# Stick-breaking scores from 128-row operands kept in place, the causal mask on VectorE, two gate columns earlier, and the squares of x summed on VectorE

## The chip, the cores and the metric

The kernel runs on one core of a Trainium2 chip. The metric is the device time of one execution in microseconds. Before the change it is 1577.78 us, the median of three runs (1577.75 to 1578.48).

In the profile PE is TensorE's matmuls, PEld its weight loads, DVE is VectorE, ACT ScalarE, POOL GpSimd and SP SyncE, which here issues most of the DMAs.

## The reference

The kernel computes one decoder block on x of 1024 tokens by 1024 channels in float32. Two mixers, stick-breaking attention (8 heads of 64) and HGRN2 (4 heads of 128), work on projections of the normalized x; sigmoid gates merge them; an output projection and a SwiGLU FFN with residuals follow. Cut to what matters here:

```python
xn = rms_norm(x, norm1_g)
proj = xn @ w_in
q_sb, k_sb, v_sb, q_hg, f_hg, i_hg, g_hg, gate_sb, gate_hg = split_cols(proj, IN_SIZES)
q = rms_norm(heads(q_sb), q_norm_g)
k = rms_norm(heads(k_sb), k_norm_g)
# stick-breaking attention, in blocks of 128 queries
z = jnp.einsum('bhtd,bhsd->bhts', qb, kb).astype(jnp.float32) * scale
causal = s_idx < t_idx
sp = jnp.where(causal, jax.nn.softplus(z), 0.0)
rest = lax.cumsum(sp, axis=3, reverse=True) - sp
w = jnp.where(causal, jnp.exp(jax.nn.log_sigmoid(z) - rest), 0.0)
outs.append(jnp.einsum('bhts,bhsd->bhtd', w.astype(vb.dtype), vb))
...
mixed = jax.nn.sigmoid(gate_sb) * y_sb + jax.nn.sigmoid(gate_hg) * y_hg
h = x + mixed @ w_out
ffn = (jax.nn.silu(hn @ w_gate) * (hn @ w_up)) @ w_down
return h + ffn
```

## The kernel before

**Precision by splitting.** Everything is kept transposed, channels on the 128 partitions and tokens along the free dimension, in two halves of 512 tokens (h = 0, 1). TensorE works on fp32r operands. To keep float32 accuracy an operand is split into a high part (rounded to fp32r) and a low part (what is left), and a product is three matmuls: high by high, high by low, low by high. So a projection column of 128 output channels is, for each half, 8 contraction tiles of three matmuls of 512 columns (tiles oh, ol for the weights, ah, al for x, pj for the PSUM bank).

**The first stage and its planner.** The stage that ends before line 782 computes the input projections and both mixers. Its instructions aren't issued in the order in which the code names them: each helper (A for ScalarE, V for VectorE, G for GpSimd, M and T for TensorE, L for a DMA on SP's queue; lines 363 to 388) records an operation with an estimated cost, and `Plan.issue` (line 124) then orders each engine's operations by a rank, and within a rank by the length of the chain of work that still hangs on them. All are issued from line 182, so the profile shows L182 for the whole stage, and groups are told apart by their tiles. The order of each engine is thus fixed when the program is built, and an engine that meets an operation whose inputs aren't ready waits there.

**Filler.** Projection columns have the lowest rank (`proj`, line 478): TensorE takes them when nothing else is ready. They form one fixed sequence, the `fill` list, built from the strings in `FILL` (line 30), one string for each of four steps u. In a string "a" stands for the q, k and v columns of the next pair of attention heads, "g" for the HGRN2 output gate of head u, "i", "f" and "q" for the other HGRN2 columns of the next head, and "G" for one of the 16 columns of the merging gates. A gate column's result is copied out of PSUM by ScalarE and stored to DRAM (sig_d) by a DMA that ScalarE issues; it is needed in the next stage. The q, k and v columns of pair u have to wait (`gate`, line 776) for marks that the pair before sets, "free q" and "free k".

**Scores** (`take`, line 516, and `scores`, line 564). Two heads of 64 channels share a tile of 128 partitions. For q each head e has a tile qs (128 by 1024): the head's own 64 partitions hold the high part of q, the other 64 hold the low part. k is split into hk and lk, where each head's 64 rows lie in its own half. For a head's scores, SP issues two DMAs that copy the head's 64 rows of hk into both halves of a tile ks. A block of scores z (128 queries by up to 512 keys) is then two matmuls: qs against ks, 128 rows deep, which gives (high q + low q) by high k; and the 64 own rows of qs against the 64 rows of lk, 64 rows deep, which gives high q by low k. A block on the diagonal has a third matmul between them, 128 columns, of an identity against a tile `never`, which adds -2^100 where the key isn't before the query. There are 96 blocks in all, 64 of them on the diagonal. Each is followed by ScalarE's Abs, Relu, Exp and Ln, a scan and a subtraction on VectorE, and ScalarE's Exp.

**Sum of squares** (`take_x`, line 445). x comes in eight tiles for each half. ScalarE squares each; the first square goes to a tile acc (shown as tail). GpSimd adds four further squares to acc for the first half and three for the second, VectorE adds up the rest and joins them. A matmul of ones against acc (ms<-tail,ones) sums over partitions, and from it comes rr, the factor that every projection result is multiplied by as it leaves PSUM.

**After the first stage** the attention and HGRN2 outputs are read back from DRAM (o_d), split, and projected (lines 787 to 823), then come the output projection and the FFN.

Of the kernel before, what the change touches and what calls it, by code (L numbers as in the profile page):

```python
# [26 lines left out]
EPS = 1e-6  # L27
NEG = -float(2.0**100)
LEVELS = [64, 32, 16, 8, 4, 2, 1]
FILL = ["GgGaifq", "gaGfiqGG", "gaGGGiqGfGG", "gGGGGG"]  # L30
BANKS = [3, 2, 3]
WARM = 9
ORDER = [1, 6, 2, 5, 7, 4, 3]
# [169 lines left out]
def hybrid_block(ctx: ExitStack, tc, xT, wi, wb, wo, wg, wu, wd, vec, outT):  # L203
# [41 lines left out]
    rst = ExitStack()  # L245
    rrp = rst.enter_context(tc.tile_pool(name="rrp", bufs=1, side="right"))
    c1 = ExitStack()
    const1 = c1.enter_context(tc.tile_pool(name="const1", bufs=1, side="right"))
    ident = const1.tile([P, P], F32, name="ident")
    ones_r = const.tile([P, P], F32R, name="ones_r")  # L250
    bones_r = const1.tile([P, P], F32R, name="bones_r")
    never = const1.tile([P, P], F32R, name="never")
    ident_r = const1.tile([P, P], F32R, name="ident_r")
    eps_t = const.tile([P, 1], F32, name="eps_t")
    one_t = const.tile([P, 1], F32, name="one_t")
    qg = const.tile([P, 1], F32, name="qg")
# [8 lines left out]
    def setup(sp):  # L265
        make_identity(nc, ident)
        t2 = sp.tile([P, P], F32, tag="t2", name="t2")
        nc.vector.memset(t2, 0.0)
        nc.vector.memset(t2[0:64, 0:64], 1.0)
        nc.vector.memset(t2[64:128, 64:128], 1.0)  # L270
        nc.vector.tensor_copy(bones_r, t2)
        nc.vector.tensor_copy(ident_r, ident)
        t3 = sp.tile([P, P], F32, tag="t3", name="t3")
        nc.gpsimd.memset(t3, NEG)
        nc.gpsimd.affine_select(
            out=t3, in_=t3, pattern=[[1, P]], compare_op=ALU.is_ge, fill=0.0,
            base=0, channel_multiplier=-1)
        nc.vector.tensor_copy(never, t3)
        nc.vector.tensor_scalar(qg, vt[:, V_Q:V_Q + 1], 0.125, None, op0=ALU.mult)
        l0, l1 = vt[:, V_LB:V_LB + 4], vt[:, V_LB + 4:V_LB + 8]  # L280
        mx = sp.tile([P, 4], F32, tag="mx", name="mx")
        e0 = sp.tile([P, 4], F32, tag="e0", name="e0")
        e1 = sp.tile([P, 4], F32, tag="e1", name="e1")
        nc.vector.tensor_tensor(mx, l0, l1, op=ALU.max)
        nc.vector.tensor_tensor(e0, l0, mx, op=ALU.subtract)
        nc.vector.tensor_tensor(e1, l1, mx, op=ALU.subtract)
        nc.scalar.activation(e0, e0, AF.Exp)
        nc.scalar.activation(e1, e1, AF.Exp)
        nc.vector.tensor_tensor(e1, e0, e1, op=ALU.add)
        nc.vector.reciprocal(e1, e1)  # L290
        nc.vector.tensor_tensor(lb, e0, e1, op=ALU.mult)
        nc.vector.tensor_scalar(omlb, lb, -1.0, 1.0, op0=ALU.mult, op1=ALU.add)
        nc.vector.tensor_scalar(nomlb, omlb, -1.0, None, op0=ALU.mult)
# [31 lines left out]
    nc.vector.memset(ones, 1.0)  # L325
    nc.vector.tensor_copy(ones_r, ones)
    setup(pp)
    pre.close()


# [2 lines left out]
    for i in range(WARM):  # L333
        nc.tensor.matmul(warm.rearrange("p (o t) -> p o t", t=P), ones_r, wide, start=i == 0,
                         stop=i == WARM - 1)


    plan = Plan()
# [6 lines left out]
        wpool: dict(w=2, oh=4, ol=4),  # L345
        psum: dict(pj=BANKS[0], z=BANKS[1], ms=BANKS[2]),
        tmpp: dict(tmp=2),
        stk: dict(hk=1, lk=1, qs=3, ks=2, vx=1, vv=1),
        att: dict(aa=8, th=2, tl=2, ww=7, ot=2, pvt=1),
        hgp: dict(xf=2, xq=2, xi=2, xg=2, kb=4, dl=2, tail=4, ql=2,  # L350
                  state=5, bl=2),
    }
# [2 lines left out]
    def new(tag, shape=(P, HALF), dt=F32):  # L355
        pool, cap = where[tag]
        plan.ring(tag, cap)
        return Buf(tag, lambda: pool.tile(list(shape), dt, tag=tag, bufs=cap, name=tag))
# [13 lines left out]
    def G(fn, *args, us, rank=0, after=(), holds=(), **kw):  # L372
        return plan.op("G", us, [(fn, args, kw)], rank, after, holds=holds)
# [71 lines left out]
    def take_x(h):  # L445
        ss, acc, ws, sqs = new("ms"), new("tail"), [[], []], []
        for k in range(KT):
            x = new("aa" if h == 0 else ("xf", "xq", "xi", "xg")[k // 2])
            load(x, xT[k][:, hs(h)], 256)
            if h == 0 and k in (0, 1, 3, 4):  # L450
                u, i = k % 3, k // 3
                n, v = fill[u]
                w = new("kb")
                load(w, wi[COL[n] + v][:, hs(i)], 256)
                ws[u].append(split_w(w))
            g = vt[:, V_N1 + k:V_N1 + k + 1]
            A(act, xh[k][h][:, hs(h)], x, AF.Copy, scale=g, aps=1, rank=2 - h)
            V(stt, xl[k][h][:, hs(h)], x, g, xh[k][h][:, hs(h)].bitcast(F32), op0=ALU.mult,
              op1=ALU.subtract, aps=1, rank=2 - h)
            if k == 0:  # L460
                A(act, acc, x, AF.Square, rank=1 - h)
            else:
                sq = new("ww")
                A(act, sq, x, AF.Square, rank=1 - h)
                sqs.append(sq)
        nv = 3 + h
        for sq in sqs[:7 - nv]:
            G(nc.gpsimd.tensor_tensor, acc, acc, sq, op=ALU.add, us=1.5, after=(last_split[0],))
        for sq in sqs[8 - nv:]:
            V(tt, sqs[7 - nv], sqs[7 - nv], sq, op=ALU.add, rank=1 - h)  # L470
        V(tt, acc, acc, sqs[7 - nv], op=ALU.add, rank=1 - h)
        M(2048, [(ss, ones, acc, True, True)])
        rstd(rr[h], ss, D, rank=1 - h)
        return ws
# [33 lines left out]
        V(stt, x, x, g, sq, op0=ALU.mult, op1=ALU.mult, aps=1)  # L508
        return x

    half = [slice(0, 64), slice(64, 128)]

    heads = [dict() for _ in range(4)]
    gains = {"q": qg, "k": vt[:, V_K:V_K + 1]}
# [1 line left out]
    def take(nm, u, h, ps):  # L516

        d = heads[u] if nm != "G" else None
        if nm == "q":
            x = qk_in(ps, gains[nm], h)  # L520
            if h == 0:
                d[nm] = [new("qs", (P, S), F32R) for _ in range(2)]
            for e, t in enumerate(d[nm]):
                hi, lo = t[half[e]][:, hs(h)], t[half[1 - e]][:, hs(h)]
                A(nc.scalar.copy, hi, x[half[e]], part=True)
                V(tt, lo, x[half[e]], hi.bitcast(F32), op=ALU.subtract, part=True)
        elif nm == "k":
            x = qk_in(ps, gains[nm], h)
            if h == 0:
                d[nm] = (new("hk", (P, S), F32R), new("lk", (P, S), F32R))  # L530
            hi, lo = d[nm][0][:, hs(h)], d[nm][1][:, hs(h)]
            A(nc.scalar.copy, hi, x, part=True)
            V(tt, lo, x, hi.bitcast(F32), op=ALU.subtract, part=True)
        elif nm == "v":
            if h == 0:
                d["v"] = new("vx", (P, S))
            V(tt, d["v"][:, hs(h)], ps, rr[h], op=ALU.mult, part=True)
        elif nm == "G":
            x = new("tmp")
            A(nc.scalar.copy, x, ps, ps=True)  # L540
            plan.op("A", 0.1, [(nc.scalar.dma_start, (sig_d[u][:, hs(h)], x), {})], lat=2.5)
        elif nm == "hi":
            y, x = new("tmp"), new("xi")
            V(tt, y, ps, rr[h], op=ALU.mult)
            tp = new("ms")
            T([(tp[:, c * P:(c + 1) * P], y[:, c * P:(c + 1) * P]) for c in range(4)],
              holds=(x,))
            A(nc.scalar.copy, x, tp, ps=True)
            d[nm, h] = x
        elif nm == "hf":  # L550
            y, x = new("tmp"), new("xf")
            V(tt, y, ps, rr[h], op=ALU.mult)
            sigmoid(x, y)
            d[nm, h] = x
        else:
            x, s = new("x" + nm[1]), new("tmp")
            V(tt, x, ps, rr[h], op=ALU.mult)
            sigmoid(s, x)
            V(tt, x, s, x, op=ALU.mult)
            d[nm, h] = x  # L560
# [3 lines left out]
    def scores(j, last):  # L564
        d = heads[j]
        for e in range(2):
            qs, ks, kl = d["q"][e], new("ks", (P, S), F32R), d["k"][1][half[e]]
            for b in range(2):
                d["free k"] = L(ks[half[b]].bitcast(F32), d["k"][0][half[e]].bitcast(F32), 256,
                                part=True, land=3.5)  # L570
            for tb in range(8):
                n = (tb + 1) * P
                prev = None
                for c0, c1 in [(0, n)] if n <= 512 else [(512, n), (0, 512)]:
                    w = c1 - c0
                    z = new("z")
                    zw = z[:, :w]
                    q = qs[:, tb * P:(tb + 1) * P]
                    diag = c1 == n
                    mms = [(zw, q, ks[:, c0:c1], True, False),  # L580
                           (zw, qs[half[e]][:, tb * P:(tb + 1) * P], kl[:, c0:c1], False, True)]
                    if diag:
                        mms.insert(1, (z[:, w - P:w], ident_r, never, False, False))
                    last = M(2 * w + P * diag, mms, after=(last,))
                    a, c, y = new("aa"), new("aa"), new("ww")
                    aw, cw, yw = a[:, :w], c[:, :w], y[:, :w]
                    A(act, aw, zw, AF.Abs, n=w, ps=True)
# [8 lines left out]
                    A(act, yw, yw, AF.Exp, n=w)  # L596
                    d["w", e, tb, c0 // 512] = y
            if e == 0:
                d["free q"] = last
        return last  # L600

    def values(j, last):
# [530 lines left out]
```

## Time and profile before

| | us |
|---|---|
| median of the runs | 1577.78 |
| profiled execution, whole | 1582.62 |
| its span | 1580.9 |
| from the start to the first scores | 57 |
| first to last score block | 57.2 to 625 |
| last store of a mixer's output | 693.6 |
| next stage's first matmuls | 744.4 |

The span is what the trace covers; the execution's own time is 1.7 us longer. A row of the order of instructions gives the start, the length, the engine, the line, the operation with "out<-in", the shapes and the count of instructions merged into the row. Matmuls are pipelined, so a matmul's length in the trace is longer than its share of the engine: what TensorE spends on one is read from its start to the start of the next. In "128*64" style shapes the first factor is the depth (rows of the array in use) and the second the columns of weights; "128x512" is the moving operand.

### The profile page before, as it was taken

What the parts mean: (1) busy time and instruction counts of PE and PEld (TensorE: products, weight loads), DVE (VectorE), ACT (ScalarE), POOL (GpSimd) and SP (SyncE); (2) the same over time, 40 slices, a digit from 0 to 9 for tenths busy, and PEclk for the clock granted to TensorE, in tenths of its full rate; (3) what the DMA queues carried; (4) which work ended last, traced back from release to release, by engine and by line L of the source; (5) the groups of instructions that cost most, each with busy time, mean ns of one, the idle gap of its engine ahead of it and who ended that gap; (6) DMA issues with size and microseconds to landing.
All of it is one profiled execution on the core that took longest, in us unless ns stands there. A gap on an engine that the chain in (4) does not pass through costs nothing.

```text
span 1580.9 us, 20525 instructions
## 1 busy us (share of the span) xinstructions
PE 1554.4 (98%) x7277; PEld 1252.4 (79%) x7277; DVE 1173.6 (74%) x1968; ACT 792.0 (50%) x1479; POOL 185.7 (12%) x207
## 2 busy tenths in 40 slices
PE   8999999999999999999999989999999999999999
PEld 5788777878788777888888868777778888778887
DVE  8798778977887667973666799888887777566553
ACT  6675768577656778462333363332233333244442
POOL 6111201101111001122441210000000000000000
PEclk9999999999999999999999999999999999999999
DMA  4211121112111311153333454666643333587672
GB/s 171 70 38 42 55 68 30 43 44 70 51 36 55 87 47 52 63 202 126 131 122 124 143 162 165 213 213 213 213 160 107 107 107 107 209 301 218 195 222 93
DMA packets 79686, 192.72 MB, mean 122 GB/s; under 512 B 9312, under 2 KB 11360, under 8 KB 78176
## 3 DMA queue, kind: packets, MB, share of 16 engines
q1 hardware_dynamic: 74976, 183.03, 35.9%
q10 hardware_dynamic: 4608, 8.39, 1.5%
q8 instruction: 57, 0.93, 0.2%
q14 instruction: 45, 0.37, 0.1%
HBM read 131.61 MB, written 55.57 MB: 118 GB/s over the span
## 4 chain that ended last, share of the span: by engine, by line
PE 81%; DVE 10%; DMA 4%; issue 2%; ACT 1%; POOL 1%; SPq 0%; DVEq 0%; ACTq 0%; POOLq 0%
PE pj L182 27%; PE f L921 19%; PE ms L182 9%; PE f L1067 4%; PE f L1069 4%; PE f L1065 4%; PE z L182 4%; PE pj L303 2%; PE pj L304 2%; PE pj L305 2%; DMA w<-wu 1%; DVE ol L238 1%; PE z L304 1%; PE z L303 1%; PE z L305 1%
## 5 line engine op out<-in xcount | busy, mean ns | idle before, releaser
L182 PE MATMUL pj<-ah,oh 128*128 128x512 f32 x704 | 290.2, 412 | 1.6 <-POOL oh L182 1.6
L182 PE MATMUL pj<-ah,ol 128*128 128x512 f32 x704 | 276.7, 393 | 0.4 <-DVE ol L182 0.4
L182 PE MATMUL pj<-al,oh 128*128 128x512 f32 x704 | 275.9, 392 | 0.9 <-DVE al L182 0.8
L921 PE MATMUL f<-fh,oh 128*128 128x512 f32 x616 | 244.2, 396 | 5.7 <-DVE g L981 2.1
L921 PE MATMUL f<-fl,oh 128*128 128x512 f32 x616 | 243.4, 395 | 0.7 <-DVE fl L851 0.7
L921 PE MATMUL f<-fh,ol 128*128 128x512 f32 x616 | 243.1, 395 | 0.0
L237 ACT CAST oh<-w 128x512 fp32r<-128x512 f32 x168 | 102.4, 620 | 197.9 <-PE f L921 128.4
L182 PEld LDWEIGHTS pj<-ah,oh 128*128 128x128 f32 x704 | 133.1, 189 | 31.1 <-issue 6.1
L182 PEld LDWEIGHTS pj<-ah,ol 128*128 128x128 f32 x704 | 132.5, 188 | 30.7 <-DVE ol L182 1.3
L182 PEld LDWEIGHTS pj<-al,oh 128*128 128x128 f32 x704 | 133.5, 190 | 23.4 <-DVE al L182 1.6
L921 PEld LDWEIGHTS f<-fh,oh 128*128 128x128 f32 x616 | 115.4, 187 | 37.1 <-DVE g L981 4.2
L238 DVE TENSOR_TENSOR ol<-w,oh 128x512 fp32r<-128x512 f32 x168 | 113.9, 685 | 40.6 <-ACT oh L237 40.3
L921 PEld LDWEIGHTS f<-fl,oh 128*128 128x128 f32 x616 | 115.5, 187 | 28.8 <-DVE fl L851 1.0
L921 PEld LDWEIGHTS f<-fh,ol 128*128 128x128 f32 x616 | 115.5, 187 | 28.2
L182 DVE TENSOR_TENSOR_SCAN aa<-aa,ww 128x512 f32<-128x512 f32 (+3 forms) x96 | 92.8, 981 | 45.8 <-ACT aa L182 34.5
L1065 PE MATMUL f<-bh,ah 128*128 128x512 f32 x296 | 114.8, 392 | 3.3 <-ACT bh L237 3.3
L1067 PE MATMUL f<-bl,ah 128*128 128x512 f32 x296 | 116.7, 394 | 1.3 <-DVE bl L238 1.3
L1069 PE MATMUL f<-bh,al 128*128 128x512 f32 x296 | 116.6, 394 | 0.0
L182 POOL TENSOR_SCALAR oh<-w 128x512 fp32r<-128x512 f32 x84 | 65.1, 775 | 426.4 <-PE pj L182 350.6
L238 DVE TENSOR_TENSOR al<-ra,ah 128x512 fp32r<-128x512 f32 x73 | 50.4, 691 | 74.8 <-ACT ah L237 74.8
L237 ACT CAST ah<-ra 128x512 fp32r<-128x512 f32 x73 | 45.5, 623 | 104.5 <-PE f L1067 103.9
L182 DVE TENSOR_TENSOR ol<-w,oh 128x512 fp32r<-128x512 f32 x84 | 59.0, 703 | 26.5 <-POOL oh L182 26.4
(276 smaller groups left out, 3025.9 us busy)
## 6 DMA issues: line engine op xcount, KB each, us to landing
w<-wi SPq DMA_DIRECT2D x42, 512.0 KB, 3.6
rb<-act_d SPq DMA_DIRECT2D x73, 256.0 KB, 4.3
w<-wg SPq DMA_DIRECT2D x22, 512.0 KB, 4.1
w<-wu SPq DMA_DIRECT2D x22, 512.0 KB, 4.1
w<-wd SPq DMA_DIRECT2D x22, 512.0 KB, 6.7
wd_d<-ds SPq DMA_DIRECT2D x44, 256.0 KB, 5.3
act_d<-c SPq DMA_DIRECT2D x11, 1024.0 KB, 3.9
act_d<-bs SPq DMA_DIRECT2D x44, 256.0 KB, 3.3
```

The costliest lines, as they stand in the source:

```text
L182: fn(*[a.real() if isinstance(a, View) else a for a in args], **{k: v.real() if isinstance(v, View) else v for k, v in kw.items()})
L237: pin(nc.scalar.copy(hi, src))
L238: pin(nc.vector.tensor_tensor(lo, src, hi.bitcast(F32), op=ALU.subtract))
L303: nc.tensor.matmul(out, hi[:, ws], a[ka][0][:, hs(h)], start=first and i == 0, stop=False)
L304: nc.tensor.matmul(out, hi[:, ws], a[ka][1][:, hs(h)], start=False, stop=False)
L305: nc.tensor.matmul(out, lo[:, ws], a[ka][0][:, hs(h)], start=False, stop=last and i == n - 1)
L921: nc.tensor.matmul(out, a[i][:, ws], bl[k][j], start=start and k == 0 and i + j == 0, stop=k == 3 and i == 1, skip_group_check=True)
L1065: nc.tensor.matmul(bank[d], hi[:, ws], bh, start=first and p == 0, stop=False, skip_group_check=True)
L1067: nc.tensor.matmul(bank[d], hi[:, ws], bl, start=False, stop=False, skip_group_check=True)
L1069: nc.tensor.matmul(bank[d], lo[:, ws], bh, start=False, stop=p == NP - 1, skip_group_check=True)
```

## The change

1. The score operands become six tiles that live through the stage. For each head e of a pair, qhh holds the high part of q in both halves, qlz the low part of q in the own half and zeros in the other, khl the high part of k in the own half and the low part in the other. The two matmuls of a block are qhh against khl (high q by high k plus high q by low k) and qlz against khl (low q by high k), both 128 rows deep. The DMA copies of k go. The tiles are single: the next pair overwrites them. ScalarE's copies for q become two for each head and half, and k is split by head.
2. The mask is no longer a matmul: VectorE writes -2^100 into the diagonal block of z in PSUM by a predicated copy, ahead of ScalarE's Abs and Relu.
3. In `FILL` one gate column moves into step 0 and one into step 1, both from the last step. "free k" is now set with "free q", after the first head's scores.
4. VectorE adds all squares of x; GpSimd adds none.
5. The buffers follow: hk, lk, qs and ks go, the ring aa grows from 8 to 10.

```diff
-FILL = ["GgGaifq", "gaGfiqGG", "gaGGGiqGfGG", "gGGGGG"]
+FILL = ["GgGGaifq", "gGaGfiqGG", "gaGGGiqGfGG", "gGGG"]
...
+    qkp = c1.enter_context(tc.tile_pool(name="qkp", bufs=1, side="right"))
...
-    never = const1.tile([P, P], F32R, name="never")
-    ident_r = const1.tile([P, P], F32R, name="ident_r")
+    future = const1.tile([P, P], I8, name="future")
+    never = const1.tile([P, P], F32, name="never")
...
-        nc.vector.tensor_copy(ident_r, ident)
-        t3 = sp.tile([P, P], F32, tag="t3", name="t3")
-        nc.gpsimd.memset(t3, NEG)
+        nc.vector.memset(never, NEG)
+        nc.gpsimd.memset(future, 1.0)
         nc.gpsimd.affine_select(
-            out=t3, in_=t3, pattern=[[1, P]], compare_op=ALU.is_ge, fill=0.0,
+            out=future, in_=future, pattern=[[1, P]], compare_op=ALU.is_ge, fill=0.0,
             base=0, channel_multiplier=-1)
-        nc.vector.tensor_copy(never, t3)
...
+    half = [slice(0, 64), slice(64, 128)]
+    qhh, qlz, khl = [[qkp.tile([P, S], F32R, name=f"{n}{e}") for e in range(2)]
+                     for n in ("qhh", "qlz", "khl")]
+    for e, t in enumerate(qlz):
+        nc.gpsimd.memset(t[half[1 - e]].bitcast(F32), 0.0)
     pre.close()
...
-        stk: dict(hk=1, lk=1, qs=3, ks=2, vx=1, vv=1),
-        att: dict(aa=8, th=2, tl=2, ww=7, ot=2, pvt=1),
+        stk: dict(vx=1, vv=1),
+        att: dict(aa=10, th=2, tl=2, ww=7, ot=2, pvt=1),
...
-        nv = 3 + h
-        for sq in sqs[:7 - nv]:
-            G(nc.gpsimd.tensor_tensor, acc, acc, sq, op=ALU.add, us=1.5, after=(last_split[0],))
-        for sq in sqs[8 - nv:]:
-            V(tt, sqs[7 - nv], sqs[7 - nv], sq, op=ALU.add, rank=1 - h)
-        V(tt, acc, acc, sqs[7 - nv], op=ALU.add, rank=1 - h)
+        for sq in sqs:
+            V(tt, acc, acc, sq, op=ALU.add, rank=1 - h)
         M(2048, [(ss, ones, acc, True, True)])
...
-        if nm == "q":
+        if nm in ("q", "k"):
             x = qk_in(ps, gains[nm], h)
-            if h == 0:
-                d[nm] = [new("qs", (P, S), F32R) for _ in range(2)]
-            for e, t in enumerate(d[nm]):
-                hi, lo = t[half[e]][:, hs(h)], t[half[1 - e]][:, hs(h)]
-                A(nc.scalar.copy, hi, x[half[e]], part=True)
-                V(tt, lo, x[half[e]], hi.bitcast(F32), op=ALU.subtract, part=True)
-        elif nm == "k":
-            x = qk_in(ps, gains[nm], h)
-            if h == 0:
-                d[nm] = (new("hk", (P, S), F32R), new("lk", (P, S), F32R))
-            hi, lo = d[nm][0][:, hs(h)], d[nm][1][:, hs(h)]
-            A(nc.scalar.copy, hi, x, part=True)
-            V(tt, lo, x, hi.bitcast(F32), op=ALU.subtract, part=True)
+            for e in range(2):
+                own, oth = half[e], half[1 - e]
+                hi = (qhh if nm == "q" else khl)[e]
+                A(nc.scalar.copy, hi[own][:, hs(h)], x[own], part=True)
+                lo = qlz[e][own] if nm == "q" else khl[e][oth]
+                V(tt, lo[:, hs(h)], x[own], hi[own][:, hs(h)].bitcast(F32), op=ALU.subtract,
+                  part=True)
+                if nm == "q":
+                    A(nc.scalar.copy, hi[oth][:, hs(h)], x[own], part=True)
...
         for e in range(2):
-            qs, ks, kl = d["q"][e], new("ks", (P, S), F32R), d["k"][1][half[e]]
-            for b in range(2):
-                d["free k"] = L(ks[half[b]].bitcast(F32), d["k"][0][half[e]].bitcast(F32), 256,
-                                part=True, land=3.5)
...
-                    mms = [(zw, q, ks[:, c0:c1], True, False),
-                           (zw, qs[half[e]][:, tb * P:(tb + 1) * P], kl[:, c0:c1], False, True)]
+                    mms = [(zw, q[e][:, tb * P:(tb + 1) * P], khl[e][:, c0:c1], q is qhh, q is qlz)
+                           for q in (qhh, qlz)]
+                    last = M(2 * w, mms, after=(last,))
                     if diag:
-                        mms.insert(1, (z[:, w - P:w], ident_r, never, False, False))
-                    last = M(2 * w + P * diag, mms, after=(last,))
+                        V(nc.vector.copy_predicated, z[:, w - P:w], future, never, n=P)
...
             if e == 0:
-                d["free q"] = last
+                d["free q"] = d["free k"] = last
```

More of the change, by code (lines that the diff above doesn't have):

```diff
@@ L335, in hybrid_block @@
                          stop=i == WARM - 1)
+    future = future.bitcast(U8)
     plan = Plan()
@@ L509, in qk_in @@
         return x
-    half = [slice(0, 64), slice(64, 128)]
+    qhh, qlz, khl = [[fixed(t) for t in ts_] for ts_ in (qhh, qlz, khl)]
     heads = [dict() for _ in range(4)]
@@ L577, in scores @@
                     zw = z[:, :w]
-                    q = qs[:, tb * P:(tb + 1) * P]
                     diag = c1 == n
-                    mms = [(zw, q, ks[:, c0:c1], True, False),
-                           (zw, qs[half[e]][:, tb * P:(tb + 1) * P], kl[:, c0:c1], False, True)]
+                    mms = [(zw, q[e][:, tb * P:(tb + 1) * P], khl[e][:, c0:c1], q is qhh, q is qlz)
+                           for q in (qhh, qlz)]
+                    last = M(2 * w, mms, after=(last,))
                     if diag:
-                        mms.insert(1, (z[:, w - P:w], ident_r, never, False, False))
-                    last = M(2 * w + P * diag, mms, after=(last,))
+                        V(nc.vector.copy_predicated, z[:, w - P:w], future, never, n=P)
                     a, c, y = new("aa"), new("aa"), new("ww")
```

## The prediction

> **What bounds the kernel now.** I read the page first, then a table of windows cut where the stages change, then the order of TensorE's instructions around single score blocks.
>
> ```profile
> span 1580.9 us, 20525 instructions
> PE 1554.4 (98%) x7277; PEld 1252.4 (79%) x7277; DVE 1173.6 (74%) x1968; ACT 792.0 (50%) x1479; POOL 185.7 (12%) x207
> ```
> ```profile
> core 0: us, PE busy (x) PEld busy (x) DVE busy (x) ACT busy (x) POOL busy (x), PEclk, DMA share, GB/s
> 0.00:57.00 57.00, 47.83 (x171) 34.41 (x171) 49.02 (x78) 33.13 (x57) 32.19 (x47) 0.94 0.44 142
> 57.00:640.00 583.00, 580.77 (x3024) 466.69 (x3025) 457.90 (x834) 419.18 (x861) 75.05 (x98) 1.00 0.18 52
> 640.00:694.00 54.00, 53.60 (x331) 46.09 (x330) 48.04 (x107) 26.62 (x48) 6.40 (x11) 1.00 0.22 67
> 694.00:744.00 50.00, 50.00 (x222) 41.36 (x221) 19.01 (x18) 20.67 (x26) 17.16 (x14) 1.00 0.59 208
> 744.00:1581.00 837.00, 822.20 (x3536) 663.86 (x3534) 599.60 (x932) 292.35 (x487) 54.94 (x38) 1.00 0.51 168
> ```
> From 57 us, where the scores begin, TensorE has work in every slice: it lacks 2.2 us of 583, then 0.4 of 54, then nothing. So a microsecond taken out of TensorE's own stream before 744 us should come off the time, as long as the others keep up. But busy is not the same as streaming, and the order shows the difference. Here is a score block off the diagonal, and one on it, each followed by a projection (pj):
>
> ```profile
> 201.52 0.39 PE L182 MATMUL pj<-ah,ol 128*128 128x512 f32 x1
> 201.75 0.39 PE L182 MATMUL z<-ks,qs 128*128 128x512 f32 x1
> 202.07 0.49 PE L182 MATMUL z<-lk,qs 64*128 64x512 f32 x1
> 202.49 0.50 PE L182 MATMUL pj<-ah,oh 128*128 128x512 f32 x1
> 202.83 0.40 PE L182 MATMUL pj<-al,oh 128*128 128x512 f32 x1
> ```
> ```profile
> 225.78 0.28 PE L182 MATMUL ms<-th,vv 128*128 128x256 f32 x1
> 225.90 0.28 PE L182 MATMUL ms<-tl,vv 128*128 128x256 f32 x1
> ...
> 231.72 0.28 PE L182 MATMUL z<-ks,qs 128*128 128x256 f32 x1
> 231.84 0.22 PE L182 MATMUL z<-never,ident_r 128*128 128x128 f32 x1
> 231.99 0.38 PE L182 MATMUL z<-lk,qs 64*128 64x256 f32 x1
> 232.30 0.50 PE L182 MATMUL pj<-ah,oh 128*128 128x512 f32 x1
> 232.64 0.39 PE L182 MATMUL pj<-al,oh 128*128 128x512 f32 x1
> ```
> Read the starts. A 512-column matmul that is 128 rows deep is followed after 0.23 us (201.52 to 201.75), a 256-column one after 0.12 (225.78 to 225.90). Around the 64-row matmul the steps are 0.32, 0.42 and 0.34 instead of 0.23 each: there are pauses going into it, in it and coming out of it. The mask matmul (never) is 128 rows deep and follows its neighbour at the normal 0.12; the pause comes only with the 64-row step behind it.
>
> **The scores on TensorE.** From 201.75 to 202.83 three 512-column matmuls take 1.08 us; at 0.23 each they are 0.69, so the pauses cost 0.39. From 231.72 to 232.64 it is 0.92 against 2 x 0.12 + 0.23 = 0.47: 0.45 for pauses and mask together.
>
> ```profile
> L182 PE MATMUL z<-lk,qs x96: 322/467/502, 57.5 to 625.4; 64*128 64x512 f32 x48, 64*128 64x128 f32 x16, 64*128 64x256 f32 x16, 64*128 64x384 f32 x16
> L182 PE MATMUL z<-never,ident_r x64: 219/222/278, 57.3 to 616.8; 128*128 128x128 f32 x64
> ```
> There are 96 blocks, 64 with a mask. 32 x 0.39 + 64 x 0.45 = 41 us; I take 42, since two blocks in a row and the narrow ones lie slightly higher. The new pair of matmuls (qhh then qlz against khl) is 128 rows deep both times and has the same columns as the old pair, so all of this goes if depth is the cause. The mask's own part of it is small: 64 x (0.45 - 0.39), 4 us.
>
> The Trainium skill speaks against this. In "TensorE: Matmul & The Clock Gate", section "Why this matters for your kernels", a single matmul of small depth takes the same time as one of 128 rows. By that rule the sum would hold only the mask. The rows above disagree: they show 0.32 and 0.42 where 0.23 is normal.
>
> **What takes the mask's place.** 64 predicated copies of 128 columns go to VectorE.
>
> ```profile
> L182 DVE COPY_PREDICATED kb<-mk,ms x48: 411/440/745, 108.9 to 682.2; 96x256 f32<-96x256 uint8 x8, 112x256 f32<-112x256 uint8 x8, 120x256 f32<-120x256 uint8 x8, 124x256 f32<-124x256 uint8 x8
> L182 DVE TENSOR_TENSOR ww<-z,aa 128x128 f32<-128x128 f32 x16 | 4.5, 280 | 0.1
> L182 ACT CAST qs<-aa x16: 604/618/626, 47.7 to 484.3; 64x512 fp32r<-64x512 f32 x16
> L182 DVE TENSOR_TENSOR lk<-aa,hk x8: 677/693/693, 44.1 to 528.8; 128x512 fp32r<-128x512 f32 x8
> ```
> The existing copies do 256 columns in 0.44 us; a 128-column VectorE operation on the same bank takes 0.28. The price of one lies between 0.28 and 0.44; I take 0.28, as the columns match: 18 us in all, up to 28. Building the operands adds 16 copies for q and 8 for k on ScalarE (24 x 0.62 = 15 us) and 8 subtractions for k on VectorE (8 x 0.69 = 5.5). Neither engine sets the pace: from 57 to 744 us VectorE is busy 458 + 48 + 19 = 525 us of 687. Afterwards it is about 549 of 645, 85%. ScalarE: 467 + 15 of 645, 75%. So this costs nothing directly, but the cover gets thinner, and each predicated copy waits for its matmuls in VectorE's queue. Behind it stand scans, weight splits (ol) and the emptying of pj banks; ScalarE's Abs waits for it, and TensorE for the banks.
>
> ```profile
> ACT aa L182 <- PE z L182: 27.3, 52, 5.3
> ```
> So far ScalarE waits 27 us in total for scores: that is room in hand. 42 us of TensorE time go, so up to 15 us more than this room may turn into TensorE waits; at best they stay at the 2.6 us of now. With the tail below I add 9, bounds 0 and 25.
>
> **What leaves the queues.** The 16 copies of k that SP issued, each with weight loads behind it, are gone.
>
> ```profile
> L182 SPq DMA_DIRECT2D ks<-hk x16: 476/587/1313, 52.6 to 530.6; - x16
> ```
> That is 16 x 0.59 = 9 us of SP's issuing. TensorE fills such waits with projections, so I count zero.
>
> **The two gate columns.** Each is 48 matmuls, 48 x 0.23 = 11 us, with its weight load on SP, two splits on GpSimd and VectorE, two copies and two stores issued by ScalarE. Moved, they add nothing; they thicken the filler for pairs 0 and 1 and thin the tail.
>
> ```profile
> 693.63 0.32 SPq L182 DMA_DIRECT2D o_d<-tail  x1
> ...
> 711.51 4.54 DVE L794 TENSOR_TENSOR ol<-o,oh 128x1024 fp32r<-128x1024 f32 x2
> ```
> After the last attention store at 693.63 the next stage's operands are ready at 716, 22 us later. The columns behind the store now cover 50 us; without two of them 28. The cover holds by 6 us; if it were gone, each microsecond short would be one of TensorE, part of the 9.
>
> **The squares of x.**
>
> ```profile
> L182 POOL TENSOR_TENSOR tail<-tail,ww x7: 1296/1698/1737, 12.9 to 31.4; 128x512 f32<-128x512 f32 x7
> 14.75 1.14 ACT L182 ACTIVATE ww<-aa 128x512 f32<-128x512 f32 x2
> 22.61 0.40 PE L182 MATMUL pj<-ah,ol 128*128 128x512 f32 x1
> 22.81 2.41 DVE L182 SCALAR_TENSOR_TENSOR al<-xq,vt,ah 128x512 fp32r<-128x512 f32 x2
> 25.14 0.68 DVE L182 TENSOR_TENSOR tail<-tail,ww 128x512 f32<-128x512 f32 x1
> 25.87 1.98 PE L182 MATMUL ms<-tail,ones 128*128 128x512 f32 x2 [2.87 <-DVE tail L182]
> ```
> The squares of the first half are there by 15.9 us. GpSimd's adds take 1.7 us each, and the last add comes on VectorE at 25.14, so TensorE stands 2.87 us before the sum. Seven adds at 0.68 are 4.8 us of VectorE in one chain; begun by 16 to 18 us it ends near 22. I take 3 us off; bounds are 0 (the adds push back the splits that TensorE reads) and 5 (the stall, and slower matmuls just after it).
>
> The set-up's new clears of qlz come ahead of GpSimd's first weight split, which now waits 3.06 us for its load; I count them at nothing, and without that cover they would push the first projection by at most the clears' own length.
>
> ```profile
> 4.85 0.62 POOL L182 TENSOR_SCALAR oh<-kb 128x512 fp32r<-128x512 f32 x1 [3.06 <-DMA kb<-wi]
> ```
> **Sum.** The profiled execution took 1582.6 us: its span and 1.7 around it. 1582.6 - 42 - 3 + 9 = 1546.6. It lies 4.8 above the median of the runs, 1577.8, so in those terms 1541.8: I say **1542**.
>
> **Rivals.**
> 1. VectorE becomes the bound. For it: 89% busy from 640 to 694 (48 of 54), and 85% overall afterwards. Against: it still has 96 us free, and moved columns lengthen the early pairs. If the new waits reach 25 us: 1577.8 - 42 - 3 + 25 = 1558.
> 2. Depth is not the cause, as the page's rule says, and the pause belongs to changing score operands. Then only mask and squares are won: 1577.8 - 4 - 3 = 1571. Against it: the mask changes operands without a pause.
> 3. Slower: operands held once. qhh, qlz and khl exist once per head of a pair, so the second head's rewriting waits for its last scores, at three changes of pair. By the rows it holds six copies at 0.62, 3.7 us per change, about 11 in all. It decides only above 15 us per change, when TensorE has no filler and the pj banks stay full; at 18 it is 1577.8 - 45 + 54 = 1587.
> 4. It does nothing: the pause moves to another instruction, because the weight load of the second matmul stays exposed. 1577.8 - 3 or so, 1576.
>
> **How the numbers follow.** Forecast 0.77, with a range of its own from 1530 (no new waits, 5 at the start) to 1558; rival 1 0.11; rival 2 0.04; rival 3 0.05; rival 4 0.03. About 0.2% (3 us) is what a measurement can tell. Faster: forecast, rivals 1 and 2, 0.92. Same: rival 4, 0.03. Slower: rival 3, 0.05. From 1528 to 1562 the range leaves out rivals 2 to 4 and the worse half of rival 1, under 0.2.
>
> **What the changed profile would show.** 192 score matmuls, all 128 deep, next start 0.23 us after a 512-column one; 7213 matmuls; the first ms<-tail near 23 us; the two-term projections of the next stage beginning near 705 instead of 744; the 837 us after it unchanged. Wrong would be: steps over 0.3 us that stay around the scores (rivals 2, 4); TensorE's idle time from 57 to 705 above 20 us, behind VectorE (rival 1) or qhh and khl (rival 3).

## The result, and the profile after

The changed kernel takes 1540.2 us (median, 1538.76 to 1541.87) against 1578.1 for the kernel before in the same session: a ratio of 0.9752, 95% interval 0.9731 to 0.9773, so 38 us or 2.5% faster. The forecast was 1542.

The head of the profile's page and the table of windows, cut where the next stage now begins:

```profile
span 1539.7 us, 20478 instructions
PE 1515.8 (98%) x7213; PEld 1242.1 (81%) x7213; DVE 1184.3 (77%) x2046; ACT 800.4 (52%) x1503; POOL 178.8 (12%) x202
```
```profile
core 0: us, PE busy (x) PEld busy (x) DVE busy (x) ACT busy (x) POOL busy (x), PEclk, DMA share, GB/s
0.00:57.00 57.00, 49.92 (x194) 37.39 (x195) 50.54 (x94) 41.13 (x75) 23.11 (x42) 0.97 0.39 132
57.00:640.00 583.00, 579.69 (x3159) 487.12 (x3158) 490.90 (x942) 431.58 (x890) 84.25 (x104) 1.00 0.16 51
640.00:704.50 64.50, 64.31 (x331) 53.95 (x330) 43.11 (x79) 32.42 (x48) 14.62 (x15) 1.00 0.47 168
704.50:1540.00 835.50, 821.89 (x3534) 663.66 (x3532) 599.76 (x933) 295.30 (x491) 56.83 (x42) 1.00 0.51 168
```
Nearly the whole gain lies ahead of the next stage, which starts 40 us sooner (704.5 instead of 744). What follows takes 835.5 us instead of 837. (The execution profiled before took 1582.6 us, 4.8 above that kernel's median of 1577.8, so the traces lie further apart than the medians.) Below, the start of the next stage is that of its first z<-oh,oh: 704.7 here, 744.6 before; its very first products, pj<-oh,oh, come 2.8 us earlier in both. TensorE's busy share is 98% both times: the share couldn't show the gain, since the pauses counted as busy. In the same 583 us between 57 and 640 TensorE now issues 3159 matmuls instead of 3024.

A score block off the diagonal, in the order of TensorE's instructions:

```profile
385.23 0.40 PE L182 MATMUL pj<-ah,ol 128*128 128x512 f32 x1
385.46 0.39 PE L182 MATMUL z<-khl,qhh 128*128 128x512 f32 x1
385.69 0.39 PE L182 MATMUL z<-khl,qlz 128*128 128x512 f32 x1
385.92 0.39 PE L182 MATMUL pj<-ah,oh 128*128 128x512 f32 x1
386.15 0.40 PE L182 MATMUL pj<-al,oh 128*128 128x512 f32 x1
```
Every step is 0.23 us; before they were 0.32, 0.42 and 0.34. The same can be read from the weight loads' waits. The first line is of the kernel before, where 59 loads of score weights stood 15.4 us in the open without waiting for any engine ("issue"). The second is of the changed kernel: those are gone, and what is left waits for VectorE to free a score bank.

```profile
PEld z L182 <- issue: 15.4, 59, 0.4
```
```profile
PEld z L182 <- DVE ww L182: 7.2, 17, 1.0
```
The first sum of squares, the mask on VectorE, and ScalarE's waits for scores:

```profile
21.34 1.13 PE L182 MATMUL ms<-tail,ones 128*128 128x512 f32 x2
```
```profile
L182 DVE COPY_PREDICATED z<-future,never 128x128 f32<-128x128 uint8 x64 | 19.2, 308 | 8.2 <-PE z L182 7.8
```
```profile
ACT aa L182 <- DVE z L182: 11.6, 16, 1.7
...
ACT aa L182 <- PE z L182: 3.1, 8, 0.9
```
The sum starts at 21.3 instead of 25.9 and TensorE no longer stands before it. The copies take 19.2 us of VectorE. ScalarE waits 3.1 us for TensorE's scores instead of 27.3, but 11.6 for the mask.

### The profile page after: what moved, and what is told of

It is laid out like the page before. It is cut to its first block, busy times and chain, and to the rows that moved or that the text cites. A ratio compares the mean times of both kernels' runs of the same rounds, so it can differ in the third digit from the quotient of the medians.

```text
span 1539.7 us, 20478 instructions
## 1 busy us (share of the span) xinstructions
PE 1515.8 (98%) x7213; PEld 1242.1 (81%) x7213; DVE 1184.3 (77%) x2046; ACT 800.4 (52%) x1503; POOL 178.8 (12%) x202
## 4 chain that ended last, share of the span: by engine, by line
PE 73%; DVE 11%; DMA 6%; ACT 4%; issue 4%; POOL 1%; SPq 1%; DVEq 0%; POOLq 0%; ACTq 0%
PE f L916 25%; PE pj L182 23%; PE ms L182 8%; PE f L1062 4%; PE f L1064 4%; PE f L1060 4%; PE z L182 2%; DMA xx<-xT 2%; DVE ol L238 1%; ACT aa L182 1%; DMA rb<-act_d 1%; POOL s L805 1%; DMA s<-sig_d 1%; DVE aa L182 1%; DVE tail L182 1%
## 5 line engine op out<-in xcount | busy, mean ns | idle before, releaser
L182 PE MATMUL pj<-ah,oh 128*128 128x512 f32 x704 | 286.7, 407 | 2.0 <-POOL oh L182 2.0
L238 DVE TENSOR_TENSOR ol<-w,oh 128x512 fp32r<-128x512 f32 x168 | 114.7, 690 | 30.0 <-ACT oh L237 29.8
L182 DVE TENSOR_TENSOR_SCAN aa<-aa,ww 128x128 f32<-128x128 f32 (+3 forms) x96 | 92.3, 975 | 33.4 <-ACT aa L182 23.8
L182 POOL TENSOR_SCALAR oh<-w 128x512 fp32r<-128x512 f32 x84 | 70.9, 844 | 394.0 <-PE pj L182 348.6
L182 ACT ACTIVATE aa<-aa 128x512 f32<-128x512 f32 (+3 forms) x128 | 69.1, 552 | 4.9 <-DVE aa L182 4.0
```

The costliest lines, as they stand in the source:

```text
L182: fn(*[a.real() if isinstance(a, View) else a for a in args], **{k: v.real() if isinstance(v, View) else v for k, v in kw.items()})
L238: pin(nc.vector.tensor_tensor(lo, src, hi.bitcast(F32), op=ALU.subtract))
```

## The experiments

The theory: the 64-row matmul is the cost, by its depth. The first rival: the pauses belong to the change of score operands or to the copied k. After that come the other parts, one at a time. Each ratio is against the kernel before on the same chip; its median there lies between 1578.1 and 1579.9 us, and times from different chips are compared no more finely than that.

**Depth alone, in the kernel before.**

```diff
-            qs, ks, kl = d["q"][e], new("ks", (P, S), F32R), d["k"][1][half[e]]
+            qs, ks, kl = d["q"][e], new("ks", (P, S), F32R), d["k"][1]
...
-                           (zw, qs[half[e]][:, tb * P:(tb + 1) * P], kl[:, c0:c1], False, True)]
+                           (zw, q, kl[:, c0:c1], False, True)]
```


> The kernel before with one edit: the second matmul of a score block takes all 128 rows of qs and lk instead of the head's own 64. (Its low term also picks up low q times the other head's low k, of rounding size.) The DMA copies of k, the mask matmul, the old squares and the old column order stay. Depth theory: the pauses of 0.39 us in each of 96 blocks go, 38 us, and about 7 us of new waits come back as in the changed kernel: 1578 - 38 + 7 = 1547, and the step after a 512-column score matmul is 0.23 us. Rival, that the pause belongs to the change of score operands or to the copied k: 1574 to 1578, steps of 0.32 and 0.42 stay.

Measured: 1549.9 us against 1578.8, ratio 0.9808 (0.9791 to 0.9824). A block of this kernel, with the old operands and the copied k:

```profile
194.81 0.39 PE L182 MATMUL z<-ks,qs 128*128 128x512 f32 x1
195.04 0.39 PE L182 MATMUL z<-lk,qs 128*128 128x512 f32 x1
195.26 0.39 PE L182 MATMUL pj<-ah,oh 128*128 128x512 f32 x1
195.49 0.39 PE L182 MATMUL pj<-al,oh 128*128 128x512 f32 x1
```
All steps are 0.23 us. The same tiles, the same queues, more rows: 29 of the 38 us. The rival falls.

The new waits don't explain why it is 29 and not 38. The next stage starts at 714.9, 29.7 us sooner than before, and up to there TensorE idles 3.9 us, against 2.6 before:

```profile
57.00:714.90 657.90, 654.01 (x3574) 551.58 (x3574) 522.10 (x958) 461.51 (x935) 100.47 (x122) 1.00 0.22 67
```
So depth takes 31 us out of TensorE's stream. The masked blocks, two thirds of all, give back less than the block read above. Here is one of 128 columns, first before and then with depth alone:

```profile
69.64 0.22 PE L182 MATMUL z<-ks,qs 128*128 128x128 f32 x1
...
70.49 0.39 PE L182 MATMUL pj<-al,oh 128*128 128x512 f32 x1
```
```profile
68.05 0.22 PE L182 MATMUL z<-ks,qs 128*128 128x128 f32 x1
68.11 0.28 PE L182 MATMUL z<-never,ident_r 128*128 128x128 f32 x1
68.22 0.27 PE L182 MATMUL z<-lk,qs 128*128 128x128 f32 x1
68.33 0.45 PE L182 MATMUL pj<-ah,oh 128*128 128x512 f32 x1
68.62 0.40 PE L182 MATMUL pj<-al,oh 128*128 128x512 f32 x1
```
It goes from 0.85 to 0.57 us, 0.28 less instead of 0.39. The masked blocks of 256 and 512 columns give back 0.33 to 0.35, so all blocks together come to an estimated 33 us; the last 2 us aren't accounted for.

**Depth undone, in the changed kernel.**

```diff
-                    mms = [(zw, q[e][:, tb * P:(tb + 1) * P], khl[e][:, c0:c1], q is qhh, q is qlz)
-                           for q in (qhh, qlz)]
+                    qc = slice(tb * P, (tb + 1) * P)
+                    mms = [(zw, qhh[e][:, qc], khl[e][:, c0:c1], True, False),
+                           (zw, qlz[e][half[e]][:, qc], khl[e][half[e]][:, c0:c1], False, True)]
```


> The changed kernel with one edit: the second matmul takes only the head's own 64 rows of qlz and khl, which gives the same sum, since the other rows of qlz are zero. Depth theory: 96 blocks pay 0.39 us again, 38 us, of which up to 7 us hides waits that are there now: 1571 to 1578. Rival, operands and queues: 1540, as the changed kernel.

Measured: 1571.2, ratio to the kernel before 0.9946 (0.9932 to 0.9961). That is 29 to 31 us above the changed kernel's two medians (1540.2, and 1542.1 in the run again below). In the trace the next stage starts 29.8 us later than in that run (734.8 against 705.0) and TensorE idles 1.3 us up to there instead of 3.6, so the shallow step adds 32 us to its stream. The steps of 0.33, 0.42 and 0.34 are back:

```profile
402.81 0.40 PE L182 MATMUL z<-khl,qhh 128*128 128x512 f32 x1
403.14 0.49 PE L182 MATMUL z<-khl,qlz 64*128 64x512 f32 x1
403.56 0.50 PE L182 MATMUL pj<-ah,oh 128*128 128x512 f32 x1
403.90 0.39 PE L182 MATMUL pj<-al,oh 128*128 128x512 f32 x1
```
**Two 64-row matmuls in a row.** What does the pause hang on?

```diff
-                           (zw, qlz[e][half[e]][:, qc], khl[e][half[e]][:, c0:c1], False, True)]
+                           *((zw, qlz[e][half[e]][:, qc], khl[e][half[e]][:, c0:c1], False, last_)
+                             for last_ in (False, True))]
```


> As the run with 64 rows in the changed kernel, but the 64-row matmul is issued twice in a row in each block (the low term is added twice, so the scores are changed a little). It tells what the pause hangs on. If it is paid once for going from 128 rows to 64 and once for going back, the second one adds only its columns: a step of 0.23 us between the two 64-row matmuls of 512 columns, about 17 us over 96 blocks, some 1590 us in all. If every 64-row matmul pays it because its weights load in the open, that step is 0.42 us and the kernel takes about 1606 us.

Measured: 1588.0, 17 us above the run with one.

```profile
396.27 0.40 PE L182 MATMUL z<-khl,qhh 128*128 128x512 f32 x1
396.59 0.73 PE L182 MATMUL z<-khl,qlz 64*128 64x512 f32 x2
397.25 0.50 PE L182 MATMUL pj<-ah,oh 128*128 128x512 f32 x1
397.59 0.39 PE L182 MATMUL pj<-al,oh 128*128 128x512 f32 x1
```
The row with x2 holds both. From the first score matmul to the second projection it is 1.32 us, against 1.09 in the block above (402.81 to 403.90). The second 64-row matmul adds 0.23 us, the plain price of its columns. So the pause is paid once for going to 64 rows and once for coming back. Neither forecast of the single step came true: between the two 64-row matmuls it is 0.33 us on average, not 0.23 and not 0.42. I read this as part of the pause showing behind the first matmul of the new depth, which no run shows by itself; the total decides.

**The changed kernel again, and three of its parts undone**, all on one chip:

> The changed kernel once more, on the same chip as the three that undo one part of it each: 1540 us.

Measured: 1542.1, ratio 0.9756 (0.9739 to 0.9773).

*The mask back on TensorE:*

```diff
...
-                    last = M(2 * w, mms, after=(last,))
                     if diag:
-                        V(nc.vector.copy_predicated, z[:, w - P:w], future, never, n=P)
+                        mms.insert(1, (z[:, w - P:w], ident_r, never, False, False))
+                    last = M(2 * w + P * diag, mms, after=(last,))
```


> The changed kernel with the mask as a matmul of 128 columns between the two score matmuls, as before the change; all three are 128 rows deep. If TensorE's stream alone counts: 64 x 0.055 us more on TensorE, 3.5 us, so 1544. Rival, that the predicated copies are what makes TensorE wait (VectorE has 64 x 0.29 = 19 us less to do here and ScalarE gets its scores sooner): the new waits of 7 us go, 1537.

Measured: 1546.2, ratio 0.9787 (0.9768 to 0.9807): 4 us more by the medians, with intervals that overlap a little; in the trace the next stage starts 5.6 us later (710.66 against 705.02), though TensorE idles 0.9 us less up to there (2.7 instead of 3.6). So the 64 mask matmuls take some 6.5 us of TensorE's stream, 0.10 each instead of the 0.055 expected. TensorE's stream counts; what relieving VectorE brings is the 0.9.

*The old column order:*

```diff
-FILL = ["GgGGaifq", "gGaGfiqGG", "gaGGGiqGfGG", "gGGG"]
+FILL = ["GgGaifq", "gaGfiqGG", "gaGGGiqGfGG", "gGGGGG"]
```


> The changed kernel with the column order of the kernel before, the two gate columns back in the last step. If TensorE has filler enough without them, and the tail's cover is only longer: 1540, within 2. Rival, that TensorE runs out of columns in the first two steps, where the q, k and v columns wait for the first head's scores: up to two columns of 11 us are lost, 1546 to 1562, with TensorE idle time before 400 us.

Measured: 1556.5, ratio 0.9862 (0.9841 to 0.9883): 14 us more. The theory that TensorE has filler enough falls here, and the rival holds. Two windows of 40 us, the granted clock inside the second, and the longest wait in the order of TensorE's instructions:

```profile
220.00:260.00 40.00, 38.21 (x198) 31.41 (x196) 36.65 (x76) 29.58 (x57) 6.57 (x8) 1.00 0.12 30
260.00:300.00 40.00, 33.92 (x186) 28.39 (x187) 38.11 (x81) 22.41 (x43) 4.01 (x6) 0.83 0.07 22
```
```profile
262.60:272.80 10.20, 8.32 (x33) 6.60 (x31) 10.16 (x21) 5.97 (x13) 0.62 (x1) 0.50 0.03 6
272.80:276.20 3.40, 0.03 (x1) 0.03 (x1) 3.40 (x7) 1.09 (x3) 0.62 (x1) 1.00 0.00 0
276.20:279.60 3.40, 3.40 (x13) 2.34 (x13) 2.18 (x4) 3.13 (x5) 0.00 (x0) 0.51 0.01 2
```
```profile
276.17 0.75 PE L182 MATMUL z<-khl,qhh 128*128 128x512 f32 x1 [3.44 <-DVE ww L182]
```
TensorE lacks 7.9 us in the two windows, and in the second one its granted clock is 0.83: half for 13.6 us. No projection starts between 256 and 277 us: there are only HGRN2 and attention pieces that hang on VectorE, which is 95% busy. At the end a score matmul waits 3.4 us for the subtraction that frees its bank. The waits cost twice, once as such and once through the clock. Up to the next stage TensorE idles 12.4 us instead of 3.6, and half the clock for 13.6 us loses 6.8; the stage starts 15.8 us later (720.8 against 705.0).

*GpSimd adding the squares again:*

```diff
-        for sq in sqs:
-            V(tt, acc, acc, sq, op=ALU.add, rank=1 - h)
+        nv = 3 + h
+        for sq in sqs[:7 - nv]:
+            G(nc.gpsimd.tensor_tensor, acc, acc, sq, op=ALU.add, us=1.5, after=(last_split[0],))
...
```


> The changed kernel with GpSimd adding seven of the squares again. If the first sum's wait is the cost: the matmul of ones starts near 25.5 us instead of 21.3, and the time is 3 to 5 us longer, 1544. Rival, that the planner's fixed order finds other work for TensorE there: 1540, no difference.

Measured: 1540.7, ratio 0.9758 (0.9741 to 0.9774): no difference that the times can tell.

```profile
25.12 1.22 PE L182 MATMUL ms<-tail,ones 128*128 128x512 f32 x1 [2.86 <-DVE tail L182]
```
The wait is back as before, and the next stage starts at 708.0 instead of 705.0. So 3 us are there at that place; but the one profiled execution of each then takes 831.3 and 835.2 us for the rest. Most of the difference is in the last (down) projection, where nothing was changed: its matmuls start over 214.9 us here, with a granted clock of 1.00 on average, and over 218.0 us at 0.98 in the changed kernel. Over all the profiled executions it varies from 214.8 to 219.4 us, the shortest at a clock of 1.00 and the longest at 0.98. The 3 us drown in that.

**The column order alone, in the kernel before** (the FILL line of the change and nothing else).

> The kernel before with the new column order alone (two gate columns moved forward). If the gate columns only make up for filler that the faster score stream uses up: nothing here, 1577 to 1580, since TensorE already has work throughout. Rival, that the order itself is better, whatever the scores do: a good part of the 14 us that it brings in the changed kernel, 1565 to 1570.

Measured: 1577.7 against 1579.1, ratio 0.9990 (0.9981 to 0.9999). That is 1.4 us by the medians and at most 3 by the interval: in the kernel as it was the order is worth next to nothing.

**One more gate column out of the tail.**

```diff
-FILL = ["GgGGaifq", "gGaGfiqGG", "gaGGGiqGfGG", "gGGG"]
+FILL = ["GgGGaifq", "gGaGfiqGG", "gaGGGiqGfGGG", "gGG"]
```


> The changed kernel with one more gate column moved from the last step into the third. Behind the last attention store stand 29 us of columns now, of which the next stage's operands need 21. One column of 11 us less leaves 18. If that cover counts: TensorE waits 3 to 5 us for the last operand before the next stage, 1544 to 1546. Rival, that the next stage starts with the operands that it has and never meets the last one late: 1541, no difference, or a little less if the column fills a gap.

Measured: 1544.1, ratio 0.9780 (0.9766 to 0.9793), between 2 and 4 us above the changed kernel's medians, with overlapping intervals. Two of the first products of the next stage:

```profile
706.72 0.40 PE L302 MATMUL z<-oh,oh 128*128 128x512 f32 x1
707.89 0.50 PE L303 MATMUL z<-ol,oh 128*128 128x512 f32 x1 [0.77 <-DVE ol L789]
```
TensorE now meets an operand (ol) that isn't split yet, and this stage takes 89.5 us instead of 86.8. The cover is real, and it was about used up: one column less costs 2.7 us there.

**Depth and VectorE's mask, in the kernel before** (the edits of the first experiment and the predicated copy, with the old order).

> The kernel before with two edits: the second matmul 128 rows deep, and the mask as a predicated copy by VectorE. The operand tiles, the DMA copies of k, the column order and the squares stay as before. If the mask's matmul is worth 4 us wherever it stands: 1550 - 4 = 1546. Rival, that the faster stream then starves under the old column order, as the changed kernel does with it: 1550 to 1560, with TensorE idle time between 200 and 300 us.

Measured: 1547.9, ratio 0.9802 (0.9788 to 0.9815), 2 us below depth alone with intervals that overlap, and between the theory's 1546 and the rival's 1550. In the traces the next stage starts 2.6 us sooner than with depth alone (712.3 against 714.9), where taking the mask off TensorE is worth 5.6 in the changed kernel. What is lost shows in the order of TensorE's instructions:

```profile
262.47 0.80 PE L182 MATMUL z<-ks,qs 128*128 128x512 f32 x1 [3.69 <-DVE ww L182]
```
It is the wait of the old column order again, at nearly the same place, with other operand tiles; 3.4 us at half the clock follow it. With depth alone, also under the old order, TensorE's longest wait between its first scores and the next stage stays under 0.8 us.

**The squares alone, in the kernel before.**

> The kernel before with the squares of x summed by VectorE alone as the only edit. If the wait ahead of the first sum is a cost of its own: the matmul of ones starts near 21.5 us instead of 25.9, the next stage starts 3 us sooner, 1575. Rival, that the time is made up again further on: the next stage starts at 744 as now, 1578 to 1580.

Measured: 1586.1 against 1579.1, ratio 1.0048 (1.0035 to 1.0062): slower by 7 us, which neither the theory nor its rival expected. The first sum starts at 21.6, as hoped, and the scores at 54.2 instead of 57.2. But the next stage starts at 751.5 instead of 744.6. The loss lies far behind the squares, in the third step:

```profile
454.96 0.79 PE L182 MATMUL z<-ks,qs 128*128 128x512 f32 x1 [3.80 <-DVE ww L182]
```
```profile
420.00:460.00 40.00, 36.11 (x194) 29.02 (x193) 35.45 (x75) 24.12 (x47) 4.48 (x6) 0.92 0.14 42
460.00:500.00 40.00, 39.12 (x197) 31.56 (x197) 29.56 (x48) 26.43 (x56) 6.24 (x9) 0.95 0.10 30
```
The planner's order shifted: between 420 and 470 us TensorE has 105 projection matmuls, against 143 in the kernel before, and none starts between 449.4 and 456.4 us. I read this as columns used up earlier. A second theory, then: what the squares alone lost is the same lack of columns, and the new order should cure it.

**Squares and column order together, in the kernel before.**

> The kernel before with two edits: the squares of x summed by VectorE, and the new column order. The squares alone made the first sum start 4 us sooner and the time 7 us longer, with a TensorE wait of 3.8 us for a score bank near 455 us and a lower granted clock around it. If what it lost is a lack of columns at that place of the fixed order: the wait goes with the new order, the next stage starts near 741 us, 1575. Rival, that the slowdown belongs to the squares whatever the order of columns: 1586, with a like wait in the third step.

Measured: 1576.5 against 1578.9, ratio 0.9980 (0.9970 to 0.9991). The same windows:

```profile
420.00:460.00 40.00, 39.99 (x216) 32.88 (x215) 36.22 (x75) 25.24 (x53) 7.68 (x9) 1.00 0.15 49
460.00:500.00 40.00, 40.00 (x231) 33.07 (x230) 33.27 (x66) 27.54 (x57) 4.44 (x7) 1.00 0.13 37
```
The wait is gone, the clock is full, and the next stage starts at 740.4. The second theory stands.

## Why the prediction was right, point by point

**The pauses (42 us with the mask).** The mechanism holds, from both sides: making the low step deep in the old kernel takes off 29 us, making it shallow in the new one adds 29 to 31. The size was put 4 to 5 us too high. In TensorE's stream depth takes 31 to 32 us where 38 was added up, and the mask 6.5 where 4 was, so 37 to 38 in place of 42. The working took the pause of a wide block without a mask for every block, and what a masked one shows beyond it for the mask; but the two blocks it read differ in width, and with depth alone a masked block gives back 0.28 to 0.35, not 0.39. The rival by which depth is not the cause is settled too. It came from the Trainium skill, "TensorE: Matmul & The Clock Gate", section "Why this matters for your kernels", where a single matmul 32 rows deep takes the time of one of 128. For 64 rows here, the second of two shallow matmuls does add the plain 0.23 us; what the rule leaves out is the change of depth. The Trainium skill's "TensorEngine Tiling (Array Packing)", section "Key Properties", says that changing the tiling mode drains TensorE. A pause of 0.4 us for going and coming back fits that; a drain as such stands in no trace here.

**The mask (4 us of it).** 4.1 by the medians, 6.5 in TensorE's stream. Its price on VectorE was put at 0.28 us; it is 0.29 in the middle and 0.31 on average, 19.2 us in all instead of 18.

**The new waits (9, bounds 0 and 25).** TensorE is idle for 3.5 us from 57 to 704.5, against 2.6 before; the longer of the remaining waits sit on score banks (7.2 us of weight loads, partly hidden). So the new waits are 1 us, and 9 was 8 too many; they stay small only with the new column order, as the next point tells. ScalarE's 27 us of room was used by about half: it waits 14.7 us for scores now, 3.1 for TensorE and 11.6 for the mask.

**The gate columns ("Moved, they add nothing").** This step was wrong. I took TensorE's filler for plentiful, because TensorE had work in every slice, and gave the thicker filler for the early pairs no worth. In the changed kernel the old order leaves a stretch without columns, and putting two of them ahead is worth 14 us. The forecast came out right because the change itself contains the cure. A fast score stream isn't the whole reason. Of the five kernels run with the old order three have a TensorE wait of 3.4 to 3.8 us on a score bank: the changed kernel with the old order, depth with VectorE's mask, and the squares alone, whose score stream is as slow as before. The kernel before and depth alone have none. Of the eight kernels run with the new order none has a wait above 0.8 us from 57 us to the next stage. Rival 1 (VectorE becomes the bound) comes nearest to the mechanism, with a chance of 0.11; it doesn't speak of filler.

**The tail.** The last attention store is at 675.8 and the last operand split ends at 697.0, 21 us later, where 22 was worked out; the columns cover 29. The margin of 7.5 us was put at 6, and the run with one column less shows that it is nearly all there was.

**The squares (3 us).** The size is right where it arises: the first sum starts at 21.3, and undoing it moves the next stage by 3.0 us. But it isn't a gain by itself: in the kernel before it costs 7 us alone and gains 2 together with the new order, and in the changed kernel's time it can't be told from nothing.

**Single operand tiles (rival 3).** No wait of TensorE on qhh, qlz or khl stands among its waits.

**The sum.** 36 us were forecast; 38 were measured by the medians, and 40 by the start of the next stage. That start is made up of 37 to 38 for depth and mask, less 1 for waits, and some 3 for the earlier first sum. The terms of 42 and 9 were both too large and enter with opposite signs, so it is partly luck that the sum came within 2 us. What the missing copies of k are worth I haven't separated. No version tried beats the changed kernel by more than its scatter.

## What to carry to other kernels

Read TensorE's pace from start to start, not from its busy share: here a lone 64-row matmul among 128-row ones cost a pause on each side, and filling its weights with zeros to 128 rows removed both without a step of its own. When a bound engine gets faster, look again at what hides its waits: filler that sufficed may run out in the middle of the stream. With an order that a planner fixes, a local gain can move a stall to a place far away, so a part is judged together with the order that it needs.

## What was unexpected of the hardware

The three runs with a long TensorE wait on a score bank also ran a part of that stretch at half the granted clock: 10.2 and 3.4 us of it in the changed kernel with the old column order, 3.4 us in depth with VectorE's mask, 10.2 us in the squares alone. The long wait isn't always what goes ahead of it. In the changed kernel with the old order the first such stretch begins at 262.6 us, behind waits of 1.5 and 0.6 us; the wait of 3.4 us comes 10 us later. In the squares alone it begins at 453.4 us, some 2.3 us into the wait.

The Trainium skill's "TensorE: Matmul & The Clock Gate", section "What's actually happening", lets the clock fall to half after an idle window of about 3.4 us. The half agrees with the 0.50 here, and in depth with VectorE's mask the fall follows a wait of 3.7 us. The other two falls came after less idle time than that, as the profile shows it, and there the measurement decides.
